# Merge gates and branch products channel by channel: all of mixer A and then all of mixer B, in place of both mixers tile by tile

## The chip, the cores and the metric

The kernel runs on one core of a Trainium2 chip. Its engines work side by side and in order: PE multiplies matrices, DVE, ACT and POOL work on vectors, SP issues the DMAs. The metric is the device time of one execution in microseconds; the kernel before takes 485.16 us (median of three runs, 485.05 to 486.32).

## The reference

A decoder layer with two token mixers over 512 tokens and 1,024 channels, all in float32. Cut to what matters here:

```python
h = rms_norm(x, norm_w[l])
proj = h @ w_in[l]          # q, k, v, z of both mixers, and gate_m (2 x 1024 channels)
o_a = moba_mixer(...)       # block sparse attention, 8 heads
o_b = nsa_mixer(...)        # compressed, selected and window attention, 8 heads
y_a = o_a * jax.nn.silu(z_a)
y_b = o_b * jax.nn.silu(z_b)
g_m = jax.nn.sigmoid(gate_m)
merged = g_m[..., :D_MODEL] * (y_a @ w_branch_a[l]) + g_m[..., D_MODEL:] * (y_b @ w_branch_b[l])
x = x + merged @ w_out[l]
```

What the change touches is the line with `merged`: 16 gate tiles of 128 channels (8 for A, 8 for B), each a product of the normed input with 128 columns of `w_in`, and 16 branch tiles, each a product of y_a or y_b (512 channels) with 128 columns of a branch weight.

## The kernel before

Every operand is split into a high and a low part in a 4-byte matmul format, and each product is three matmuls (high by high, low by high, high by low). The helper `mm3` (L314) issues them all, so nearly every product has the line L325 and is told apart by its result tile: pgt and pgc are projections, pbr is a branch product, po the output product. A gate tile is 8 chunks of the input, so 24 matmuls of 512 columns; a branch tile is 4 chunks of y, so 12 matmuls.

The program is written by a planner that runs when the kernel is built. It keeps a clock of its own and four generators that yield the cost of what they issue: `attention`, `gemms`, `cmp` and `x_rms`. The main loop (L1281) lets the ready generator with the least time so far go on, and delays what follows a product (chains of steps on DVE, ACT and POOL) until the modelled result is there. So PE's order is a mixture of attention and of the projections: where the attention waits for a softmax, products of `gemms` stand between. A generator that waits for something (`need`, `room`, a chain's `ready`) is passed over until the planner's clock has reached it. When attention has nothing but its own steps left and `gemms` is waiting, PE's order holds attention alone.

Attention is 24 units: 8 heads of mixer A, then 16 of mixer B (two for each head, of which the second adds to the first one's result O). A unit has scores (sps, L845 and L846), DVE's addition of the bias with a running minimum (L864), ACT's exponential (L879), DVE's reciprocal (L882), POOL's scaling of the probabilities P (L883), transposes on PE (pt, L892), the split into ph on ACT (L904) and pl on DVE (L906), and the products O with the values (L926). The products of a unit stand beside the scores of the next. After a head, ACT and DVE copy O out (ot L951, ys L955); after two heads DVE and ACT multiply by the silu gate and split the result (L965 to L967): the tiles yh and yl. Four pairs of them make up y of a mixer.

`gemms` (L1176) gives the projections in a fixed order, the z gates last. Then come the gates and branches. A gate (`gmgate`) is `gemm_chan` (24 matmuls into a PSUM buffer of the pool "g", which has two), then on DVE a multiplication with the token's norm (L1156) and on ACT a tanh (L1157). A branch is 12 matmuls into another buffer of "g" and DVE's (g + 1) * pbr (L1222), for which it needs all four y of its mixer. When both branches of a tile j are there, DVE adds them (L1226), ACT and DVE split the sum (L1227, L1228) into mh and ml, and after the last j the output product po runs.

Before: five gates of A first (`NGM = 5`). Then for every j: the gates of j that are still missing (B's, and from j = 5 on A's too), the branch of A, the branch of B, the sum.

Weights come through a stream `W` in the order in which the products use them: one DMA per tile of 256 KB, a split into wh (ACT or POOL, L296 or L298) and wl (DVE or POOL, L300). `ahead` (L493) sets how many tiles are split ahead, up to four.

Of the kernel before, what the change touches and what calls it, by code (L numbers as in the profile page):

```python
# [15 lines left out]
ALU = mybir.AluOpType  # L16
# [3 lines left out]
D = 1024  # L20
DH = 64
P = 128
# [12 lines left out]
POFF = [0, 128, 384, 768]  # L35
WT = 560
NATT = 35
NGM = 5
NW = 8
NRAW = 4  # L40
NWARM = 28
# [46 lines left out]
def hybrid_kernel(ctx: ExitStack, tc: tile.TileContext, x, xT, norm_w, wtok, wchan, gains, w1,  # L88
# [14 lines left out]
    def nm(s):  # L103
        uid[0] += 1
        return f"{s}{uid[0]}"
# [4 lines left out]
    now = [0.0]  # L110
# [26 lines left out]
    def cm(n):  # L137
        return 4.5 + 0.4427 * n
# [94 lines left out]
    def psum(tag, name, dt=F32):  # L233
        return alloc(tag, name, dt=dt)
# [9 lines left out]
    def room(*tags):  # L244

        def f():
            r = 0.0
            for tag in tags:
                if len(held[tag]) >= RES[tag][1]:
                    t = [z[0] for z in held[tag] if z[0] is not None]  # L250
                    if not t:
                        return None
                    r = max(r, min(t))
            return r
        return f

    def need(*names):
        def f():
            t = [done.get(n) for n in names]
            return None if None in t else max(t)  # L260
        return f
# [52 lines left out]
    def mm3(dst, sts, mvs, rows=1, start=True, stop=True):  # L314

        n = len(sts)
        cost = cm(dst.shape[-1]) * rows
        for k in range(0, n, rows):
            ks = range(k, k + rows)
            cs = {id(z[2]): z[2] for i in ks for z in (sts[i], mvs[i]) if z[2]}.values()  # L320
            if cs:
                yield all_of(*cs)
            for a, b in ((0, 0), (1, 0), (0, 1)):
                for i in ks:
                    nc.tensor.matmul(dst, sts[i][a], mvs[i][b], start=(start and i == a == b == 0),  # L325
                                     stop=(stop and i == n - 1 and b == 1))
                if rows > 1 or b:
                    yield cost if rows > 1 else 3 * cost
# [143 lines left out]
    def chan_tiles(name):  # L472
        return [(wchan[cnames.index(name), i], 512) for i in range(2)]
# [3 lines left out]
    tiles = []  # L477
    for n_ in ORDER_T:
        tiles += tok_tiles(n_) if n_ in tlay else chan_tiles(n_)
    for j in range(NGM):  # L480
        tiles += chan_tiles(f"gm{j}")
    for j in range(8):
        for w in range(2):
            if w or j >= NGM:
                tiles += chan_tiles(f"gm{8 * w + j}")
        tiles += [(wbr[j, i], 512) for i in range(2)]
    for c in range(4):
        tiles += [(wout[c, i], 512) for i in range(4)]
    W = Stream(tiles, NRAW - 1, lambda: wp.tile([P, WT], F32R, name=nm("wh"), tag="whi"),
               lambda: wp.tile([P, WT], F32R, name=nm("wl"), tag="wlo"))  # L490
    W1 = Stream([(w1[kv, q], 512) for kv in range(2) for q in range(8)], 1, lambda: att("vh"), lambda: att("vl"))

    def ahead(f):  # L493

        W.split(W.i + min(4, int(f * 4 + 0.8)))
# [442 lines left out]
    yhl = {}  # L938
# [211 lines left out]
    gms = {}  # L1150

    def gmgate(w, j):
        t = att("gm", F32)

        def emit(ps):
            c = Chain(now[0] + 230).do({"D": 602}, lambda e: e.tensor_mul(t, ps, R), ps)  # L1156
            gms[w, j] = t, c.do({"A": ca(512)}, lambda e: e.activation(t, t, AF.Tanh, scale=0.5))  # L1157
        yield from gemm_chan(f"gm{8 * w + j}", emit)

    def load_consts():  # L1160
        c = Chain(dma(ident, consts[:, :P], 512))
        c.do({"P": 547}, lambda e: e.tensor_copy(identr, ident)).mark("ident")
        dma(gn, bass.AP(tensor=gains.tensor, offset=gains.offset, ap=[[0, P], [1, 6 * DH]]), 1536)
        dma(rel, relone[:, :16], 64)
        o = alloc("gmt", "oh", (64, S))
        oh.append(att("oh"))
        c = Chain(dma(o, relone[:, 16:], 1024))
        c.do({"A": ca(512)}, lambda e: e.copy(oh[0][:64, :], o), o)
        c.do({"A": ca(16)}, lambda e: e.copy(relr, rel))
        c.do({"D": 82}, lambda e: e.tensor_sub(relr[32:64, :], rel[32:64, :], relr[32:64, :].bitcast(F32))).mark("oh")  # L1170
        t = dma(cst[:, P:], consts[:, P:], 2000)
        c = Chain(t)
        for i in (0, 2):
            c.do({"D": 102}, lambda e, i=i: e.tensor_scalar_mul(gn[:, i, :], gn[:, i, :], 0.125))

    def gemms():  # L1176
        yield from proj_v("v0", True)
        yield from proj_norm("qk0", 0, "ttgg")
        yield from bias_rows()
        yield from x_rows()  # L1180
        yield from proj_norm("qk1", 0)
        yield from compress_w(0)
        yield from compress_w(1)
        yield from proj_norm("qk2", 0)
        yield from proj_v("v1")
        yield from proj_norm("qk3", 0)
        yield from proj_norm("qb0", 2)
        yield from proj_norm("kb", 4)
        yield from proj_v("vb")
        yield from zgate("a", 0)  # L1190
        yield from zgate("a", 1)
        yield from proj_norm("qb1", 2)
        yield from zgate("a", 2)
        yield from zgate("a", 3)
        for j in range(4):
            yield from zgate("b", j)
        for j in range(NGM):
            yield from gmgate(0, j)
        xr = {}
        ms = []  # L1200
        for j in range(8):
            for w in range(2):
                if (w, j) not in gms:
                    yield from gmgate(w, j)
            ws = W.take(2, P)
            if j == 6:
                for t in range(0, NT, 2):
                    yield room("P")
                    xp = alloc("P", "xr", (P, 1280))
                    for i in range(2):  # L1210
                        xr[t + i, 0] = xp[:, i * 512:(i + 1) * 512]
                        dma(xr[t + i, 0], x[(t + i) * P:(t + i + 1) * P, :512], 2048)
            c = []
            for w in range(2):
                yield need(*((("y", "ab"[w], k) for k in range(4))))
                yield room("g")
                ps = psum("g", "pbr")
                yield from mm3(ps, ws[4 * w:4 * w + 4], [yhl["ab"[w], k] for k in range(4)])
                ahead((w + 1) / 2)
                g, gc = gms[w, j]  # L1220
                yield gc.ready
                c.append(Chain(max(now[0] + 230, gc.t)).do({"D": 602}, lambda e, g=g, ps=ps: e.scalar_tensor_tensor(  # L1222
                    g, g, 1.0, ps, op0=ALU.add, op1=ALU.mult), ps))
            g0, g1, a, b = gms[0, j][0], gms[1, j][0], att("mh"), att("ml")
            ch = c[1]
            ch.do(either(512), lambda e, g0=g0, g1=g1: e.tensor_add(g0, g0, g1))  # L1226
            ch.do({"A": ca(512)}, lambda e, g0=g0, a=a: e.copy(a, g0))  # L1227
            ch.do(either(512), lambda e, g0=g0, a=a, b=b: e.tensor_sub(b, g0, a.bitcast(F32)))  # L1228
            ms.append((a, b, ch))
        for c in range(4):  # L1230
            ws = W.take(4, 256)
            if c == 0:
                for t in range(NT):
                    xr[t, 1] = att("xr", F32)
                    dma(xr[t, 1], x[t * P:(t + 1) * P, 512:], 2048)
            st = [[(a[:, t * P:(t + 1) * P], b[:, t * P:(t + 1) * P], ch) for a, b, ch in ms] for t in range(NT)]
            pss_ = {}
            for t in range(NT):
                if c == 0 and t == 0:

                    for i in range(2):
                        yield room("g")
                        pss_[i] = psum("g", "po")
                        yield from mm3(pss_[i][:, :256], st[i][:7], ws[:7], stop=False)
                if t in pss_:
                    yield from mm3(pss_[t][:, :256], st[t][7:], ws[7:], start=False)
                    ps = pss_[t]
                else:
                    yield room("g")
                    ps = psum("g", "po")  # L1250
                    yield from mm3(ps[:, :256], st[t], ws)
                ahead((t + 1) / NT)
                xv = xr[t, c // 2][:, (c % 2) * 256:(c % 2 + 1) * 256]
                ch = Chain(now[0] + 230).do({"D": 335}, lambda e, xv=xv, ps=ps: e.scalar_tensor_tensor(
                    xv, ps[:, :256], 0.25, xv, op0=ALU.mult, op1=ALU.add), ps)
                ch.call(lambda t=t, c=c, xv=xv: dma(out[t * P:(t + 1) * P, c * 256:(c + 1) * 256], xv, 1024))
# [24 lines left out]
    while any(r.live for r in runs):  # L1281
        live = [r for r in runs if r.live]
        ws = [(r, r.wait()) for r in live]
# [86 lines left out]
```

## Time and profile before

| | |
|---|---|
| median of three runs | 485.16 us (485.05 to 486.32) |
| profiled execution | 486.89 us, of which the span is 485.1 us |
| mean granted clock of PE | 0.996 |
| busy: PE / DVE / ACT / POOL | 475.4 / 338.4 / 256.6 / 159.0 us |
| chain that ended last | PE 95%, DVE 2%, DMA 1% |

The profile is one execution. Busy time is a share of the whole span. Ends of matmuls are modelled, so that a 512-column matmul is shown with 0.39 us while the next one starts 0.23 us after it: the pace of PE is read from the starts. The chain of waits follows the work that ended last backwards, and its pieces add up to the span. A wait names the instruction that came last of those waited for.

### The profile page before, as it was taken

To read this page: it belongs to the slowest core of one execution; us is meant where nothing else is said; L and a number is where in the kernel's file an instruction comes from. 1 tells how busy PE (TensorE), PEld (TensorE's weight loads), DVE (VectorE), ACT (ScalarE), POOL (GpSimd) and SP (SyncE) were. 2 spreads that over 40 slices of the span, in tenths; PEclk is the share of its full clock that TensorE was granted. 3 is DMA by queue.
4 is the path that set the end of the run, shared out by engine and by line. 5 is a ranking of instruction groups with operands and counts; after the bars stand their busy time and mean duration, and the time that the engine had idled before them with its cause. 6 is when DMAs were issued, how large, how long until landed. Compare 5 with 4: busy or idle time off the path is not lost.

```text
span 485.1 us, 8685 instructions
## 1 busy us (share of the span) xinstructions
PE 475.4 (98%) x3060; PEld 426.7 (88%) x3060; DVE 338.4 (70%) x862; ACT 256.6 (53%) x631; POOL 159.0 (33%) x211
## 2 busy tenths in 40 slices
PE   7999999999999999999999999998999999999997
PEld 7999899999999989888888888886788888889997
DVE  5888999688898589797788677775555535444331
ACT  7656695477675286766686477764222231222210
POOL 0165577165555025465440254354000000000000
PEclk9999999999999999999999999998999999999999
DMA  8737243544344224122212221211133324526421
GB/s 275 221 74 171 61 134 112 151 114 135 79 123 140 74 66 113 41 65 68 65 45 75 84 68 57 49 42 45 43 106 112 94 81 139 166 76 217 142 89 43
DMA packets 28124, 49.15 MB, mean 101 GB/s; under 512 B 3313, under 2 KB 5745, under 8 KB 28081
## 3 DMA queue, kind: packets, MB, share of 16 engines
q1 hardware_dynamic: 28080, 48.60, 34.8%
q8 instruction: 24, 0.39, 0.4%
q14 instruction: 20, 0.16, 0.1%
HBM read 45.84 MB, written 2.75 MB: 100 GB/s over the span
## 4 chain that ended last, share of the span: by engine, by line
PE 95%; DVE 2%; DMA 1%; issue 0%; ACT 0%; POOL 0%; SPq 0%; DVEq 0%
PE pgc L325 30%; PE pgt L325 21%; PE po L325 9%; PE pbr L325 9%; PE O L926 6%; PE pt L892 6%; PE sps L845 3%; PE sps L846 3%; PE pgf L523 3%; PE pq L777 2%; PE hps L692 1%; DMA wr<-in_wtok 1%; PE hps L691 1%; PE scp L1014 1%; PE O L1070 0%
## 5 line engine op out<-in xcount | busy, mean ns | idle before, releaser
L300 DVE TENSOR_TENSOR wl<-wr,wh 128x512 fp32r<-128x512 f32 (+1 forms) x118 | 83.0, 712 | 7.3 <-ACT wh L296 7.0
L325 PE MATMUL pgc<-hh,wh 128*128 128x512 f32 x208 | 84.5, 406 | 0.0
L325 PE MATMUL pgt<-wh,hh 128*128 128x256 f32 (+1 forms) x288 | 82.6, 287 | 0.3 <-DVE v L608 0.3
L325 PE MATMUL pgc<-hh,wl 128*128 128x512 f32 x208 | 81.9, 394 | 0.0
L325 PE MATMUL pgc<-hl,wh 128*128 128x512 f32 x208 | 81.8, 393 | 0.0
L325 PE MATMUL pgt<-wl,hh 128*128 128x256 f32 (+1 forms) x288 | 81.2, 282 | 0.0
L325 PE MATMUL pgt<-wh,hl 128*128 128x256 f32 (+1 forms) x288 | 81.0, 281 | 0.0
L296 ACT CAST wh<-wr 128x512 fp32r<-128x512 f32 (+1 forms) x90 | 54.0, 616 | 27.5 <-DMA wr<-in_wout 21.9
L883 POOL TENSOR_SCALAR P<-P,sst,gate 128x512 f32<-128x512 f32 (+3 forms) x56 | 40.5, 727 | 62.8 <-DVE sst L882 46.8
L298 POOL TENSOR_SCALAR wh<-wr 128x512 fp32r<-128x512 f32 (+1 forms) x34 | 23.3, 687 | 114.9 <-DMA wr<-in_wchan 70.3
L864 DVE CUSTOM_DVE_ANT_0 sb<-sps,T 128x512 f32<-128x512 f32 (+3 forms) x96 | 46.0, 484 | 17.7 <-PE sps L846 16.6
L325 PEld LDWEIGHTS pgt<-wh,hh 128*128 128x128 f32 x288 | 54.3, 188 | 1.2 <-DVE v L608 0.5
L325 PEld LDWEIGHTS pgt<-wh,hl 128*128 128x128 f32 x288 | 54.2, 188 | 0.3
L325 PEld LDWEIGHTS pgt<-wl,hh 128*128 128x128 f32 x288 | 54.3, 188 | 0.0
L879 ACT ACTIVATE P<-sb,sst 128x512 f32<-128x512 f32 (+3 forms) x88 | 50.9, 580 | 6.3 <-DVE sst L864 6.0
L904 ACT CAST ph<-pt 128x512 fp32r<-128x512 f32 (+2 forms) x72 | 33.5, 477 | 26.0 <-PE pt L892 25.3
L325 PEld LDWEIGHTS pgc<-hl,wh 128*128 128x128 f32 x208 | 39.1, 188 | 9.1
L325 PEld LDWEIGHTS pgc<-hh,wh 128*128 128x128 f32 x208 | 39.1, 188 | 6.8
L325 PEld LDWEIGHTS pgc<-hh,wl 128*128 128x128 f32 x208 | 39.2, 188 | 6.7
L892 PE MATMUL pt<-cst,P 128*128 128x128 f32 x232 | 41.8, 278 | 0.3 <-POOL P L883 0.3
L906 DVE TENSOR_TENSOR pl<-pt,ph 128x512 fp32r<-128x512 f32 (+2 forms) x72 | 38.5, 548 | 4.1 <-ACT ph L904 3.7
L370 POOL TENSOR_TENSOR nr<-nss,mhalf 128x4 f32<-128x4 f32 x28 | 32.3, 1157 | 21.4 <-DVE nss L369 19.4
(208 smaller groups left out, 1076.6 us busy)
## 6 DMA issues: line engine op xcount, KB each, us to landing
wr<-in_wchan SPq DMA_DIRECT2D x52, 256.0 KB, 2.7
wr<-in_wtok SPq DMA_DIRECT2D x36, 256.0 KB, 2.8
T<-rtab SPq DMA_DIRECT2D x16, 256.0 KB, 3.8
wr<-in_w SPq DMA_DIRECT2D x16, 256.0 KB, 2.7
wr<-in_wbr SPq DMA_DIRECT2D x16, 256.0 KB, 2.6
wr<-in_wout SPq DMA_DIRECT2D x16, 256.0 KB, 2.9
x<-in_xT SPq DMA_DIRECT2D x8, 256.0 KB, 5.2
xr<-in_x SPq DMA_DIRECT2D x8, 256.0 KB, 4.4
```

The costliest lines, as they stand in the source:

```text
L296: e.copy(hi, raw)
L298: e.tensor_scalar(hi, raw, 1.0, 1.0, op0=ALU.mult, op1=ALU.mult)
L300: c.do(either(n), lambda e, hi=hi, lo=lo, raw=raw: e.tensor_sub(lo, raw, hi.bitcast(F32))).mark((w, 1, i))
L325: nc.tensor.matmul(dst, sts[i][a], mvs[i][b], start=(start and i == a == b == 0), stop=(stop and i == n - 1 and b == 1))
L370: c.do({"p": 430 + 150 * w}, lambda e: e.tensor_tensor(v(dst), v(ss), mhalf[:parts, :w], op=ALU.pow))
L864: e.tensor_tensor_reduce(z["sb"][:, :L], sps[:, :L], T[:, S - L:], scale=-1.0, scalar=3e38, op0=ALU.add, op1=ALU.min, accum_out=st[:, 0, b ...
L879: e.activation(pv(), z["sb"][:, :L], AF.Exp, bias=st[:, 0, b:b + 1], scale=-1.0, accum_out=st[:, 1, b:b + 1])
L883: c.do({"P": 315 + 0.834 * L}, lambda e: e.tensor_scalar(pv(), pv(), st[:, 2, b:b + 1], g, op0=ALU.mult, op1=ALU.mult))
L892: nc.tensor.transpose(pt[:, (b - kb) * P:(b - kb + 1) * P], u.p0 if u.p0 is not None and b == 0 else u.pb[:, POFF[b] + kb * P:POFF[b] + (k ...
L904: e.copy(z["w"][0], pt[:, :w])
L906: ch.do({"D": cd(w)}, lambda e: e.tensor_sub(z["w"][1], pt[:, :w], z["w"][0].bitcast(F32)), pt)
L926: nc.tensor.matmul(O[0][:, S - n:], v.bitcast(F32) if kb == 3 else v, w, start=(u.first and kb == 0 and i == 0), stop=(u.last and kb == 3 ...
```

## The change

The gates and branches of all eight tiles of mixer A come first, gate and branch in turn; then those of mixer B, each followed by the sum of its tile. The five gates ahead are gone. The branch is a generator function of its own. It takes one weight tile at a time instead of two, and calls `ahead` after each of its four chunks of y instead of once per branch. The weight stream has the same tiles in the new order. The numbers of instructions of each kind on PE stay as they are.

```diff
--- before.py
+++ after.py
@@ -35,7 +35,6 @@
 POFF = [0, 128, 384, 768]
 WT = 560
 NATT = 35
-NGM = 5
 NW = 8
 NRAW = 4
 NWARM = 28
@@ -477,13 +476,9 @@
     tiles = []
     for n_ in ORDER_T:
         tiles += tok_tiles(n_) if n_ in tlay else chan_tiles(n_)
-    for j in range(NGM):
-        tiles += chan_tiles(f"gm{j}")
-    for j in range(8):
-        for w in range(2):
-            if w or j >= NGM:
-                tiles += chan_tiles(f"gm{8 * w + j}")
-        tiles += [(wbr[j, i], 512) for i in range(2)]
+    for w in range(2):
+        for j in range(8):
+            tiles += chan_tiles(f"gm{8 * w + j}") + [(wbr[j, w], 512)]
     for c in range(4):
         tiles += [(wout[c, i], 512) for i in range(4)]
     W = Stream(tiles, NRAW - 1, lambda: wp.tile([P, WT], F32R, name=nm("wh"), tag="whi"),
@@ -1157,6 +1152,23 @@
             gms[w, j] = t, c.do({"A": ca(512)}, lambda e: e.activation(t, t, AF.Tanh, scale=0.5))
         yield from gemm_chan(f"gm{8 * w + j}", emit)
 
+    def branch(w, j):
+
+        ws = W.take(1, P)
+        yield need(*((("y", "ab"[w], k) for k in range(4))))
+        yield room("g")
+        ps = psum("g", "pbr")
+        i = 0
+        for c in mm3(ps, ws, [yhl["ab"[w], k] for k in range(4)]):
+            yield c
+            if not callable(c):
+                i += 1
+                ahead(i / 4)
+        g, gc = gms[w, j]
+        yield gc.ready
+        return Chain(max(now[0] + 230, gc.t)).do({"D": 602}, lambda e: e.scalar_tensor_tensor(
+            g, g, 1.0, ps, op0=ALU.add, op1=ALU.mult), ps)
+
     def load_consts():
         c = Chain(dma(ident, consts[:, :P], 512))
         c.do({"P": 547}, lambda e: e.tensor_copy(identr, ident)).mark("ident")
@@ -1194,15 +1206,13 @@
         yield from zgate("a", 3)
         for j in range(4):
             yield from zgate("b", j)
-        for j in range(NGM):
-            yield from gmgate(0, j)
         xr = {}
         ms = []
         for j in range(8):
-            for w in range(2):
-                if (w, j) not in gms:
-                    yield from gmgate(w, j)
-            ws = W.take(2, P)
+            yield from gmgate(0, j)
+            yield from branch(0, j)
+        for j in range(8):
+            yield from gmgate(1, j)
             if j == 6:
                 for t in range(0, NT, 2):
                     yield room("P")
@@ -1210,19 +1220,8 @@
                     for i in range(2):
                         xr[t + i, 0] = xp[:, i * 512:(i + 1) * 512]
                         dma(xr[t + i, 0], x[(t + i) * P:(t + i + 1) * P, :512], 2048)
-            c = []
-            for w in range(2):
-                yield need(*((("y", "ab"[w], k) for k in range(4))))
-                yield room("g")
-                ps = psum("g", "pbr")
-                yield from mm3(ps, ws[4 * w:4 * w + 4], [yhl["ab"[w], k] for k in range(4)])
-                ahead((w + 1) / 2)
-                g, gc = gms[w, j]
-                yield gc.ready
-                c.append(Chain(max(now[0] + 230, gc.t)).do({"D": 602}, lambda e, g=g, ps=ps: e.scalar_tensor_tensor(
-                    g, g, 1.0, ps, op0=ALU.add, op1=ALU.mult), ps))
+            ch = yield from branch(1, j)
             g0, g1, a, b = gms[0, j][0], gms[1, j][0], att("mh"), att("ml")
-            ch = c[1]
             ch.do(either(512), lambda e, g0=g0, g1=g1: e.tensor_add(g0, g0, g1))
             ch.do({"A": ca(512)}, lambda e, g0=g0, a=a: e.copy(a, g0))
             ch.do(either(512), lambda e, g0=g0, a=a, b=b: e.tensor_sub(b, g0, a.bitcast(F32)))
```

On PE, the order differs first behind gate 0 of mixer A (pgc_4018). Before:

```order
L325 MATMUL pgc_4018<-hh,wh_3942 128x512
L325 MATMUL pgc_4018<-hh,wl_3943 128x512
L325 MATMUL pgc_4018<-hl,wh_3942 128x512
L325 MATMUL pgc_4110<-hh,wh_4030 128x512
L325 MATMUL pgc_4110<-hh,wl_4031 128x512
L325 MATMUL pgc_4110<-hl,wh_4030 128x512
L325 MATMUL pgc_4110<-hh,wh_4030 128x512
```

After:

```order
L324 MATMUL pgc_4018<-hh,wh_3942 128x512
L324 MATMUL pgc_4018<-hh,wl_3943 128x512
L324 MATMUL pgc_4018<-hl,wh_3942 128x512
L324 MATMUL pbr_4109<-yh_2753,wh_4030 128x512
L324 MATMUL pbr_4109<-yh_2753,wl_4031 128x512
L324 MATMUL pbr_4109<-yl_2754,wh_4030 128x512
L324 MATMUL pbr_4109<-yh_2957,wh_4030 128x512
```

Before, the next product is gate 1 of A (pgc_4110); now it is branch 0 of A (pbr_4109), and gate 1 comes 12 matmuls later.

On PE, the last two attention units: the last product of the older one (pf), the transposes of the last one, its products, and its compressed part (ch). Before:

```order
L926 MATMUL O_4962<-pf_4971,vb_2659 128x128
L892 MATMUL pt_4986<-cst,p_4893 128x128
L892 MATMUL pt_4986<-cst,P_4900 128x128 x3
L892 MATMUL pt_4991<-cst,P_4900 128x128 x3
L892 MATMUL pt_4998<-cst,P_4900 128x128 x2
L926 MATMUL O_4962<-ph_4995,vb_2521 128x512
L926 MATMUL O_4962<-pl_4996,vb_2521 128x512
L892 MATMUL pt_5012<-cst,P_4900 128x128
L926 MATMUL O_4962<-ph_5001,vb_2572 128x384
L926 MATMUL O_4962<-pl_5002,vb_2572 128x384
L926 MATMUL O_4962<-ph_5004,vb_2612 128x256
L926 MATMUL O_4962<-pl_5005,vb_2612 128x256
```

After, from the older unit's last but one gate matmul on:

```order
L324 MATMUL pgc_4869<-hl,wh_4810 128x512
L921 MATMUL O_4980<-pf_4990,vb_2659 128x128
L887 MATMUL pt_4998<-cst,p_4907 128x128
L887 MATMUL pt_4998<-cst,P_4917 128x128 x3
L887 MATMUL pt_5003<-cst,P_4917 128x128 x3
L887 MATMUL pt_5010<-cst,P_4917 128x128 x2
L324 MATMUL pbr_5013<-yh_2753,wh_4849 128x512
L324 MATMUL pbr_5013<-yh_2753,wl_4850 128x512
L324 MATMUL pbr_5013<-yl_2754,wh_4849 128x512
L324 MATMUL pbr_5013<-yh_2957,wh_4849 128x512
L324 MATMUL pbr_5013<-yh_2957,wl_4850 128x512
L324 MATMUL pbr_5013<-yl_2958,wh_4849 128x512
```

Before, no gate or branch matmul stands here. Now three of a gate (pgc_4869, of which the last is shown) stand before the older unit's last product, and nine of branch 4 of A (pbr_5013, six are shown) behind the transposes. Three more follow before the last two products of attention. The last row of attention, ch, has the number 2065 on PE before and 2089 now.

On DVE, from the second but last scores of the last unit to its transposes' split: sb are scores, pl the low part of transposed probabilities, gm a gate, wl a weight's low part. Before:

```order
L864 ISA sb_4936,sst_4873<-sps_4924,T_4710 128x384
L864 ISA sst_4873 128x1
L906 TENSOR_TENSOR pl_4929<-pt_4919,ph_4928 128x512
L864 ISA sb_4954,sst_4873<-sps_4938,T_4710 128x256
L864 ISA sst_4873 128x1
L1222 SCALAR_TENSOR_TENSOR gm_4017<-gm_4017,pbr_4853 128x512
L906 TENSOR_TENSOR pl_4943<-pt_4932,ph_4942 128x384
L300 TENSOR_TENSOR wl_4951<-wr_4761,wh_4950 128x512
L882 RECIPROCAL sst_4873<-sst_4873 128x1
L906 TENSOR_TENSOR pl_4958<-pt_4945,ph_4957 128x256
L882 RECIPROCAL sst_4873<-sst_4873 128x1
L906 TENSOR_TENSOR pl_4996<-pt_4986,ph_4995 128x512
```

After:

```order
L859 ISA sb_4952,sst_4889<-sps_4940,T_4714 128x384
L859 ISA sst_4889 128x1
L901 TENSOR_TENSOR pl_4945<-pt_4935,ph_4944 128x512
L859 ISA sb_4967,sst_4889<-sps_4954,T_4714 128x256
L859 ISA sst_4889 128x1
L901 TENSOR_TENSOR pl_4959<-pt_4948,ph_4958 128x384
L877 RECIPROCAL sst_4889<-sst_4889 128x1
L901 TENSOR_TENSOR pl_4971<-pt_4961,ph_4970 128x256
L877 RECIPROCAL sst_4889<-sst_4889 128x1
L1151 TENSOR_TENSOR gm_4868<-pgc_4869,R 128x512
L901 TENSOR_TENSOR pl_5008<-pt_4998,ph_5007 128x512
```

Before, a branch's evacuation (gm_4017) and a weight split (wl_4951) stand between the last scores (sb_4954) and the last reciprocal; now neither does, and a gate's evacuation (gm_4868) stands behind the last reciprocal.

## Rows read from the trace of the kernel before

**Rows 1.** The page: busy us of PE, and the last chain by engine.
```profile
PE 475.4 (98%) x3060; PEld 426.7 (88%) x3060; DVE 338.4 (70%) x862; ACT 256.6 (53%) x631; POOL 159.0 (33%) x211
...
PE 95%; DVE 2%; DMA 1%; issue 0%; ACT 0%; POOL 0%; SPq 0%; DVEq 0%
```

**Rows 2.** The waits of PE over the whole span: total us, times, longest.
```profile
PE O L926 <- DVE pl L906: 1.3, 3, 0.6
...
PE pbr L325 <- ACT yh L966: 0.7, 1, 0.7
...
PE pt L892 <- POOL P L883: 0.3, 1, 0.3
```

**Rows 3.** Windows of 25 us: busy us (matmuls) by engine, granted clock, DMA.
```profile
300.00:325.00 25.00, 25.00 (x148) 21.88 (x146) 19.59 (x66) 18.34 (x54) 11.13 (x17) 1.00 0.21 54
325.00:350.00 25.00, 22.76 (x102) 17.51 (x101) 13.35 (x30) 10.73 (x25) 5.89 (x9) 0.93 0.13 43
350.00:375.00 25.00, 25.00 (x110) 20.30 (x109) 13.70 (x23) 5.61 (x10) 1.71 (x2) 1.00 0.33 95
```

**Rows 4.** Windows of 2 us, same columns.
```profile
334.00:336.00 2.00, 2.00 (x8) 1.32 (x7) 1.49 (x3) 0.98 (x4) 0.54 (x1) 0.53 0.00 0
```

**Rows 5.** Timeline of PE, 328 to 341 us: start, us, line, operation, [idle before it <-who ended it].
```profile
328.36 0.48 PE L926 MATMUL O<-ph,vb 128*128 128x512 f32 x1
329.08 0.50 PE L926 MATMUL O<-pl,vb 128*128 128x512 f32 x1 [0.24 <-DVE pl L906]
...
332.46 1.97 PE L892 MATMUL pt<-cst,P 128*128 128x128 f32 x8 [0.27 <-POOL P L883]
...
336.80 0.40 PE L325 MATMUL pbr<-yh,wh 128*128 128x512 f32 x1
...
340.79 0.39 PE L325 MATMUL pgc<-hh,wh 128*128 128x512 f32 x1
```

**Rows 6.** The chain of waits, 320 to 345 us: start, us, engine and line.
```profile
322.64 0.46 PE O L926 x2
...
323.34 0.11 PE pt L892
323.45 0.35 PE O L926 x2
...
324.49 0.46 PE O L926 x4
324.94 0.23 PE O L1070
...
327.02 0.44 PE pt L892 x4
...
331.21 1.21 POOL P L883 x2
...
340.95 4.19 PE pgc L325 x18
```

**Rows 7.** Timeline of DVE, 322 to 331 us.
```profile
322.58 0.68 DVE L1156 TENSOR_TENSOR gm<-pgc,R 128x512 f32<-128x512 f32 x1
...
329.28 0.68 DVE L1222 SCALAR_TENSOR_TENSOR gm<-gm,pbr 128x512 f32<-128x512 f32 x1
...
330.35 0.68 DVE L300 TENSOR_TENSOR wl<-wr,wh 128x512 fp32r<-128x512 f32 x1
```

**Rows 8.** Timeline of all engines, 428 to 444 us.
```profile
429.75 0.40 PE L325 MATMUL pbr<-yh,wh 128*128 128x512 f32 x1
...
429.95 0.69 DVE L1156 TENSOR_TENSOR gm<-pgc,R 128x512 f32<-128x512 f32 x1 [2.91 <-PE pgc L325]
...
438.05 0.39 PE L325 MATMUL po<-wl,mh 128*128 128x256 f32 x1 [0.24 <-DVE wl L300]
```

**Rows 9.** Instructions on gm: duration ns min/median/max, first and last start.
```profile
L1156 DVE TENSOR_TENSOR gm<-pgc,R x16: 627/692/693, 266.8 to 430.0; 128x512 f32<-128x512 f32 x16
...
L1222 DVE SCALAR_TENSOR_TENSOR gm<-gm,pbr x16: 681/689/690, 329.3 to 435.5; 128x512 f32<-128x512 f32 x16
```

## The prediction

> **What bounds the kernel now.** I read the page first, then the waits of PE, the windows, the timeline and the chain. The page shows a PE that is busy for 98% of the span, with 95% of the chain that ended last on it [rows 1]. So only time that PE loses can be won. The waits of PE name the losses: a product of probabilities and values, O, waiting for pl (three times), a branch product waiting for yh, a transpose waiting for P [rows 2]. All three lie between 325 and 345 us; the only other wait of any size is the start's, for the first weights, which the change does not reach. The windows show the same: from 325 to 350 us PE ran 102 matmuls at a granted clock of 0.93, in the next 25 us 110 at 1.00 [rows 3], and from 334 to 336 us the clock stood at 0.53, about the lower of its two levels, 1.2 GHz [rows 4].
>
> Recorded waits understate the loss, because a PE that idles between two starts counts as busy while the first drains. So I price the stretch by starts. It begins at 328.36, when the scores of the last attention unit are issued and nothing from the gate stream is left, and ends at 340.79, when the next gate starts: 12.43 us [rows 5]. Its content at full rate comes from the unit just before, which had filler [rows 6]. One set of products: 0.46 + 0.11 + 0.35 + 0.46 = 1.38 us. There are two sets, one of them with L1070 (0.23), so 2.99 us. Nine transposes at 0.44 / 4 = 0.11 us, 0.99 us. Twelve branch matmuls at 4.19 / 18 = 0.233 us each, 2.79 us. Sum 6.77 us. **The loss is 12.43 - 6.77 = 5.7 us**, in three parts: 328.36 to 332.46 (4.10 us against 1.38) loses 2.7, waiting for P; 332.46 to 336.80 (4.34 against 2.60) loses 1.7, waiting for pl and at the low clock; 336.80 to 340.79 (3.99 against 2.79) loses 1.2, waiting for the last y of mixer B.
>
> The cause is in the code. The gate stream runs beside attention as its filler. After gate (1,0) and branch (0,0) it meets branch (1,0), which needs all four y of B, and the last of these needs attention's last head. From then on attention runs alone on PE, one dependent step after the other.
>
> **The change part by part.** Nothing is removed or added: as many matmuls as before, the same gates, branches and weight tiles, the same arithmetic on DVE, ACT and POOL. Only places move. The order starts to differ behind gate 0 of A, whose result DVE takes at 266.8 us [rows 9]; nothing before that can change.
>
> 1. The branches of A become filler. They need y of A alone, finished with the eighth of 24 attention units. PE's order shows the end of attention after 24 more gate or branch matmuls than before (its last row of attention stands at 2089 instead of 2065): 24 x 0.233 = 5.6 us of work moved ahead, against a loss of 5.7 us. In before none stands between the last unit's scores and its last product. In after six stand between the scores and the older unit's products, three before the last unit's transposes, nine behind those and three before the last two products.
>
> 2. What is late next, by the three parts of the loss. For pl: nine matmuls, 2.1 us, stand where PE lost 1.7; nothing should remain. For y: gate 5 and branch 5 of A, gates and branches 6 and 7, and gate 0 of B stand before the first branch of B, 24 + 12 + 36 + 36 + 24 = 132 matmuls or 30.8 us; nothing remains. For P: it came 4.10 us after 328.36. In after PE has six matmuls, the older unit's products and three more matmuls in that place, 1.40 + 1.38 + 0.70 = 3.5 us. At the chain's present length 0.6 us would remain. But the chain should be shorter: in before DVE does a branch evacuation (0.68) and a weight split (0.68) inside it [rows 7], and in DVE's new order neither stands there. So 0 to 0.6 us; I take 0.2.
>
> 3. Evacuation. A gate or branch holds one of two PSUM buffers, so a gate's buffer must be free again 12 matmuls (2.8 us) after its end. In before this already happens at every j: the gate of B is followed by two branches, and the second takes the gate's buffer. DVE starts on it 0.2 us into the next product and needs 0.69 us [rows 8]; PE shows no wait there. Under attention DVE is later, but the 12 matmuls are spread over more time too: before the starved stretch the last gate was taken at 322.58 [rows 7], and no product waited for its buffer. Cost 0; if the cover were gone, each turn could cost up to one evacuation, 0.69 us.
>
> 4. DVE gets about three more evacuations of 0.68 us under attention and two more weight splits, some 3.4 us over the 60 us from 267 to 327 us, where over a fifth of it is free (19.59 of 25 us busy from 300 to 325) [rows 3]. The bounds: from 0 (PE does not wait for DVE there now) to the three waits of the last unit, 1.3 us [rows 2], in each of the eight units of the stretch, 10.4 us. I take 0.1, near the first: each unit keeps about as many gate and branch matmuls beside it by PE's order (before 48, 9, 18, 9, 15, 9, 18, 9, after 45, 9, 18, 9, 15, 12, 15, 15), so that the unit is no less covered.
>
> 5. Weights. One tile per 12 matmuls, in the same ratio as before for gates and branches; loads are only reordered. In the seam to the output product PE waits 0.24 us for a weight split [rows 8]. Now `ahead` runs after each quarter of a branch, so that on DVE three of the first four splits of the output weights stand ahead of the last branch's evacuation, where two stood. It may gain 0.24 us, or lose as much; I take a gain of 0.1.
>
> Sum: 5.7 - 0.2 - 0.1 + 0.1 = 5.5 us. The profiled execution took 486.89 us with a span of 485.1; the sum acts on the span, which becomes 479.6. The median of the runs is 485.16, so the forecast is **479.7 us**.
>
> A rule speaks against the new rhythm. The clock is 1.00 from 350 to 375 us, where one gate alternates with two branches [rows 3]. The Trainium skill ("TensorE: Matmul & The Clock Gate", "A second HAM failure mode: psum-queue depth-cycling") says that a stream of 512-column products which turns through PSUM buffers can idle briefly at every turn, and that the clock then falls again and again. By that the turns of one gate and one branch would cost clock from 341 to 435 us and the gain would be gone; by the row they cost nothing and the sum stands.
>
> **Rivals.** (a) *P stays late.* The chain from scores to P keeps its 4.1 us or grows, since POOL scales two tiles in a row (1.21 us) [rows 6] and the unit before must finish first; then PE idles, the clock falls as now, and only the parts for pl and y, 1.7 + 1.2, are won, less 0.3: 485.16 - 2.6 = 482.6. For it: it is the largest part of the loss. Against: nine matmuls stand in this place, and two steps less in the chain.
>
> (b) *DVE falls behind, the result is slower.* The new evacuations delay pl in the units that were covered so far. The price is point 4's upper end: 10.4 us in eight units, 485.16 - 5.5 + 10.4 = 490.1; in six units 487.5. It decides from (5.5 + 1.5) / 8 = 0.9 us a unit. For it: DVE is the busiest engine behind PE and works in order. Against: PE waits nowhere for it from 250 to 325 us, and the page's 70% leave room.
>
> (c) *The turns cost clock.* If from 341 to 435 us the clock were 0.93, as in the starved window [rows 3], the 94 us would grow by 0.07 x 94 = 6.6 us: 485.16 - 5.5 + 6.6 = 486.3, no difference that can be told. Against: 1.00 from 350 to 375 us, with the same two buffers and turns after 12 matmuls. This is the outcome that the Trainium skill's rule above would give.
>
> (d) *The change fills nothing*, because the planner holds the branches back: 485.2. The order excludes it, as far as an order can.
>
> **How the numbers follow.** Forecast 82%, with its own range of 478.9 to 481.3 (at best the whole 5.7 and the seam's 0.24, with 0.3 us for the spread of the sum; at worst P 0.4 us later still and one more unit with the last one's 1.3 us of waits). (a) 10%, (b) 5%, (c) 2%, (d) 1%. A measurement of this kernel tells about 0.3%, 1.5 us, from no change. Forecast and (a) are faster: 0.92. (c), (d) and a mild (b): same 0.04. The rest of (b): slower 0.04. The range that holds eight in ten takes in (a) as well: 478.8 to 482.8.
>
> **What would show it.** Right: the waits of PE for pl, P and yh between 325 and 345 us are gone or below 0.5 us in sum; the granted clock is 1.00 in every window there; the chain has pgc and pbr where POOL P, ot, ys and yh stood; the span ends near 479.6. Step 2 is wrong if a transpose still waits for P; step 3 if pgc or pbr waits for an evacuation of gm; step 4 if O waits for pl before 315 us. The forecast as a whole is wrong if the clock drops behind 341 us or new waits of PE exceed 1 us in sum.

## The result, and the profile after

The changed kernel takes 480.76 us (median of four runs, 479.29 to 481.04) against 485.74 us (485.05 to 487.58): a ratio of 0.9881 with a 95% interval of 0.9858 to 0.9904. Beside the experiments it ran once more: 480.38 us against 485.83 us, ratio 0.989 (0.9871 to 0.9909). Both say 5.0 to 5.5 us, a good 1%. The forecast was 479.7 us.

The page of the changed kernel, the lines that answer to [rows 1]:

```profile
span 478.9 us, 8690 instructions
...
PE 471.8 (99%) x3060; PEld 425.8 (89%) x3060; DVE 339.0 (71%) x862; ACT 254.8 (53%) x628; POOL 159.7 (33%) x214
...
PE 97%; DVE 1%; DMA 1%; ACT 0%; SPq 0%; issue 0%; DVEq 0%
```

Its waits of PE, all of them (who waited for whom: us in total, times, longest), to be held against [rows 2]:

```profile
PE pgf L518 <- ACT wh L295: 2.1, 1, 2.1
PE pw L385 <- POOL ones L337: 0.9, 1, 0.9
PE pgt L324 <- DVE v L603: 0.3, 1, 0.3
PE hps L687 <- DVE vl L299: 0.2, 1, 0.2
PE po L324 <- DVE xr L1253: 0.2, 1, 0.2
```

The three waits of the starved stretch, for pl, yh and P, are gone, and so is the wait for a weight split in front of the output product [rows 8]. What is left stands in front of the stretch or behind it. The windows (busy us and matmuls by engine, granted clock, DMA) that answer to [rows 3]:

```profile
325.00:350.00 25.00, 25.00 (x129) 21.04 (x128) 14.24 (x31) 10.70 (x27) 5.65 (x10) 1.00 0.25 76
350.00:375.00 25.00, 25.00 (x110) 20.36 (x109) 11.11 (x17) 5.61 (x10) 1.85 (x3) 1.00 0.33 95
```

From 325 to 350 us PE now runs 129 matmuls where it ran 102, at a granted clock of 1.00 in place of 0.93. The chain of waits through the last attention unit (start, us, engine and line), which in before ran through DVE, POOL and ACT [rows 6]:

```profile
329.12 0.12 PE sps L841
329.24 0.22 PE pt L887 x2
329.46 1.39 PE pgc L324 x6
330.86 0.46 PE O L921 x2
331.32 0.11 PE pt L887
331.43 0.59 PE O L921 x4
332.02 0.70 PE pgc L324 x3
332.72 0.22 PE O L921 x2
332.94 0.98 PE pt L887 x9
333.93 2.09 PE pbr L324 x9
336.01 0.46 PE O L921 x2
...
338.08 0.24 PE O L1065
338.32 5.55 PE pgc L324 x24
```

Every piece is PE's, each starts where the one before it ends, and nine transposes take 0.98 us, where the prediction counted 0.99. From the start of the first product to the start of what follows attention's last one, what took 8.44 us without filler in before (328.36 to 336.80) takes 7.46 us here, with fifteen filler matmuls inside (330.86 to 338.32). The seam to the output product runs through as well:

```profile
427.04 2.76 PE pbr L324 x12
429.80 5.34 PE po L324 x45
```

### The profile page after: what moved, and what is told of

It is laid out like the page before. It is cut to its first block, busy times and chain, and to the rows that moved or that the text cites. A ratio compares the mean times of both kernels' runs of the same rounds, so it can differ in the third digit from the quotient of the medians.

```text
span 478.9 us, 8690 instructions
## 1 busy us (share of the span) xinstructions
PE 471.8 (99%) x3060; PEld 425.8 (89%) x3060; DVE 339.0 (71%) x862; ACT 254.8 (53%) x628; POOL 159.7 (33%) x214
## 4 chain that ended last, share of the span: by engine, by line
PE 97%; DVE 1%; DMA 1%; ACT 0%; SPq 0%; issue 0%; DVEq 0%
PE pgc L324 30%; PE pgt L324 21%; PE po L324 9%; PE pbr L324 9%; PE O L921 6%; PE pt L887 6%; PE sps L840 3%; PE sps L841 3%; PE pgf L518 3%; PE pq L772 2%; PE hps L687 1%; PE hps L686 1%; DMA wr<-in_wtok 1%; PE scp L1009 1%; PE O L1065 0%; PE pct L1052 0%
## 5 line engine op out<-in xcount | busy, mean ns | idle before, releaser
L299 DVE TENSOR_TENSOR wl<-wr,wh 128x512 fp32r<-128x512 f32 (+1 forms) x118 | 84.2, 717 | 10.3 <-ACT wh L295 10.1
L295 ACT CAST wh<-wr 128x512 fp32r<-128x512 f32 (+1 forms) x87 | 51.9, 617 | 25.1 <-DMA wr<-in_wout 19.3
L887 PE MATMUL pt<-cst,P 128*128 128x128 f32 x232 | 40.7, 272 | 0.0
```

What stands on the lines that cost most here:

```text
L295: e.copy(hi, raw)
L299: c.do(either(n), lambda e, hi=hi, lo=lo, raw=raw: e.tensor_sub(lo, raw, hi.bitcast(F32))).mark((w, 1, i))
L887: nc.tensor.transpose(pt[:, (b - kb) * P:(b - kb + 1) * P], u.p0 if u.p0 is not None and b == 0 else u.pb[:, POFF[b] + kb * P:POFF[b] + (k ...
```

## The experiments

Two theories stood. *Filler*: the gain is the work that PE can do while attention's last units wait for their own steps. *Rhythm*: the gain comes from gate and branch in turn, with weights taken one tile at a time. The first four kernels leave the rhythm of before as it is and change only what stands in reach of attention. For each, the stretch that the edits can touch is read from two starts: the last matmul of the compressed scores (scp, in front of the first difference) and the first output product (po). Up to scp PE's order is the same in all these kernels, and still that start differs by up to 2 us between executions, so the stretch behind it is finer than the whole time. The first four were timed beside the kernel before in the table's first row, the last four and the changed kernel beside one of 485.83 us (484.26 to 486.1); each ratio is to the one beside it.

| kernel | time, us (range) | ratio to before (95%) | last scp to first po, us |
|---|---|---|---|
| before | 485.64 (484.63 to 486.93) | | 435.3 - 261.9 = 173.4 |
| changed, again | 480.38 (479.68 to 480.57) | 0.989 (0.9871 to 0.9909) | 429.1 - 261.6 = 167.5 |
| four gates ahead | 489.14 (488.56 to 490.27) | 1.0071 (1.0047 to 1.0096) | 437.1 - 261.0 = 176.1 |
| six gates ahead | 482.49 (482.16 to 483.53) | 0.9929 (0.9904 to 0.9954) | 431.8 - 261.9 = 169.9 |
| eight gates ahead | 479.88 (479.2 to 481.19) | 0.9881 (0.9854 to 0.9908) | 428.8 - 260.9 = 167.9 |
| B reads y of A | 480.35 (479.94 to 481.18) | 0.989 (0.9867 to 0.9913) | 428.9 - 261.4 = 167.5 |
| B first | 503.03 (502.87 to 503.19) | 1.0359 (1.0331 to 1.0387) | 451.6 - 260.9 = 190.7 |
| evacuation in two steps | 479.34 (478.91 to 480.48) | 0.9879 (0.9855 to 0.9903) | 427.9 - 260.2 = 167.7 |
| split ahead once | 481.09 (480.69 to 481.86) | 0.9909 (0.9889 to 0.9929) | 428.1 - 260.5 = 167.6 |

**Four, six and eight gates ahead**, in the kernel before:

```diff
-NGM = 5
+NGM = 4      # and 6, and 8
```

> The kernel before with four gates of mixer A ahead of the tiles instead of five; the rhythm of gate, gate, branch, branch stays. Theory (filler): attention's end now stands 24 matmuls earlier on PE (last row 2041, before 2065), so the last two units run with no gate or branch matmul beside them instead of one; 24 x 0.233 = 5.6 us more are left for after it, and PE idles for as long: 5.6 us slower than before, up to 8 where the lower clock lasts longer, 490.5 to 494 us. Rival (rhythm: the gain comes from gate and branch in turn, one weight tile at a time, in the stretch after attention): that rhythm is as in before, so no change, 485 to 486 us.

> The kernel before with six gates of mixer A ahead instead of five. Theory (filler): attention's last row moves to 2089 as in the changed kernel, 24 matmuls stand between the last scores and it, so the waits for P and pl go. But the first branch of B stands right behind attention, so the wait for the last y (1.2 us) stays: 485.5 - 4.4 = 481.1 us, 480.5 to 482. Rival (rhythm): no change, 485 to 486 us.

> The kernel before with all eight gates of mixer A ahead; gate, branch, branch behind. Theory (filler): 24 matmuls between the last scores and attention's last row, and more than 24 behind it ahead of the first branch of B, so all three waits go: as fast as the changed kernel, 479.3 to 480.8 us, with a span near 479. Rival (rhythm): no change, 485 to 486 us, since the branches still stand in pairs with two weight tiles at a time.

One constant moves the time from 489.1 over 485.6 and 482.5 to 479.9 us, and with eight gates ahead the kernel before is as fast as the changed one. The rhythm is out: nothing of it was changed. Two sizes were missed. With four gates it lost 3.5 us and not 5.6. Its waits of PE:

```profile
PE pt L892 <- POOL P L883: 3.4, 3, 1.7
...
PE O L926 <- DVE pl L906: 1.1, 4, 0.4
```

PE waited longer, but attention also ended sooner: its last product (L1070) starts at 333.0, 72.0 us after the last scp, in before at 336.5, 74.6 us after it. Of these 2.6 us, 0.8 are the clock's: it fell in before and did not fall here. Here is its window (granted clock 1.00), and then PE's transposes of the last unit's P and the first matmul behind attention:

```profile
325.00:350.00 25.00, 23.04 (x109) 17.85 (x110) 13.70 (x29) 9.20 (x22) 3.43 (x6) 1.00 0.13 42
```

```profile
329.79 1.09 PE L892 MATMUL pt<-cst,P 128*128 128x128 f32 x8 [0.26 <-POOL P L883]
...
333.32 0.40 PE L325 MATMUL pbr<-yh,wh 128*128 128x512 f32 x1
```

These are the same matmuls as in before, alone on PE in both. They take 3.53 us here (329.79 to 333.32) and took 4.34 in before (332.46 to 336.80, [rows 5]), so of the 1.7 us that the prediction's second part loses, 0.8 belong to the low clock and 0.9 to the waits. What is left of the 2.6 us, 1.8, is filler that had only held attention up. So a missing filler matmul costs its time only where the chain beside it is the longer one.

With six gates the waits for P and pl are gone and one wait is left, for the last y, with more than it had cost in before: the twelve matmuls of B's first branch take 4.86 us from start to start (338.08 to 342.94), a loss of 2.1 us where before lost 1.2. The end of attention in its chain of waits:

```profile
338.43 1.29 DVE wl L300 x2
339.72 0.03 issue
339.75 0.69 DVE ys L955
340.45 0.02 issue
340.47 0.70 DVE ys L965
341.18 0.02 issue
341.20 0.63 ACT yh L966
341.82 0.04 issue
341.87 1.23 PE pbr L325 x3
```

Two weight splits stand on DVE in front of the steps that make y, and only nine matmuls of B's first branch are behind attention to cover them. That is the price of filler that reaches only to attention's last row: 482.5 in place of 479.9 us with two gates more.

**The branches of B read y of A**, in the kernel before:

```diff
-                yield need(*((("y", "ab"[w], k) for k in range(4))))
+                yield need(*((("y", "a", k) for k in range(4))))
...
-                yield from mm3(ps, ws[4 * w:4 * w + 4], [yhl["ab"[w], k] for k in range(4)])
+                yield from mm3(ps, ws[4 * w:4 * w + 4], [yhl["a", k] for k in range(4)])
```

> The kernel before, in which the branches of B read y of A (the output is then not the layer's: mixer B's attention is computed but not merged). Nothing else changes: five gates ahead, gate, branch, branch. Theory (filler): what stopped the stream of gates and branches was the need for y of B; without it the stream goes on under attention's tail and all 5.7 us of loss go: 479.3 to 480.8 us, no wait of PE for P, pl or yh. Rival (rhythm): no change, 485 to 486 us.

480.35 us, and no wait for P, pl or yh is left. All that was taken away is the need for mixer B's last head, so this need is what stopped the stream.

**B first**, in the changed kernel (the two loops and the weight stream change places):

```diff
         for j in range(8):
-            yield from gmgate(0, j)
-            yield from branch(0, j)
+            yield from gmgate(1, j)
+            yield from branch(1, j)
         for j in range(8):
-            yield from gmgate(1, j)
+            yield from gmgate(0, j)
...
-            ch = yield from branch(1, j)
+            ch = yield from branch(0, j)
```

> The changed kernel with the mixers swapped: gates and branches of all tiles of B first, then those of A. The rhythm and the number of instructions stay. Theory (filler): branch 0 of B waits for attention's end, so only one gate is left as filler for the last eight units, which had 165 matmuls of it (38 us) in the changed kernel and have 9 now; about 36 us of PE work moves behind attention. Each of these units then loses what the last one lost in the kernel before (2.7 + 1.7 us, more where the scores wait too): 480 + 8 x 4.4 = 515 us, 505 to 525. Rival (rhythm): as fast as the changed kernel, 479 to 481 us.

503.03 us: the same rhythm and the same instructions, 22.7 us slower than the changed kernel. The direction is the filler's; the size was set too high. Two views of it, the waits of PE and the windows:

```profile
PE pt L887 <- POOL P L878: 4.6, 7, 1.4
PE O L921 <- DVE pl L901: 3.5, 11, 0.6
PE pct L1052 <- DVE pcs L1039: 3.2, 1, 3.2
```

```profile
275.00:300.00 25.00, 20.53 (x118) 15.23 (x116) 19.53 (x75) 19.05 (x59) 10.07 (x17) 1.00 0.14 35
300.00:325.00 25.00, 20.26 (x110) 14.68 (x109) 17.00 (x59) 16.15 (x50) 9.77 (x17) 1.00 0.00 1
```

The waits for P and pl come back all along the row of units and not only in the last; the one for pct stands once, in front of the row. Attention's last product starts at 322.6, 61.7 us after the last scp, in the changed kernel run beside it at 337.3, 75.6 us after it. So 156 matmuls or 36.3 us of work were taken out and attention ran 13.9 us faster without them: 22.4 us of loss, close to the measured 22.7. The expectation had priced each unit by the last one, which is alone on PE; inside the row, the next unit's scores still stand beside it, which is read from the order and was not tested by itself.

**The branch's evacuation in two steps**, in the changed kernel:

```diff
-        return Chain(max(now[0] + 230, gc.t)).do({"D": 602}, lambda e: e.scalar_tensor_tensor(
-            g, g, 1.0, ps, op0=ALU.add, op1=ALU.mult), ps)
+        c = Chain(max(now[0] + 230, gc.t)).do({"D": 602}, lambda e: e.tensor_scalar_add(g, g, 1.0))
+        return c.do({"D": 602}, lambda e: e.tensor_mul(g, g, ps), ps)
```

> The changed kernel with the branch's evacuation on DVE in two instructions (g + 1, then times the product) instead of one: 16 more DVE instructions, up to 0.69 us each, some 5 of them under attention. Theory (filler): DVE has more than a fifth of its time free there, and PE is covered; within 0.5 us of the changed kernel, 479.3 to 481.3 us, and no wait of PE for gm, pl or P. Rival (DVE is close to its limit under attention, so that the moved evacuations are as many as it bears): five units lose up to 1.3 us each, 483 to 487 us.

479.34 us, with no wait of PE for gm, pl or P. It is no faster by its edit: the stretch behind scp is 167.7 us, the changed kernel's 167.5, and its profiled execution reached scp 1.4 us earlier, in front of all that the edit touches. Up to attention's last product DVE bears four more steps (0.41 to 0.97 us each) than in the changed kernel, so the rival in which DVE falls behind is out.

**Split ahead once at a branch's end**, in the changed kernel:

```diff
             if not callable(c):
                 i += 1
-                ahead(i / 4)
+        ahead(1)
```

> The changed kernel with the weight stream asked to split ahead once at the end of each branch (four tiles) instead of after each quarter of it. Theory: the quarters matter only at the seam to the output product, where the kernel before waited 0.24 us for a weight split; at most that wait comes back, 479.3 to 481.3 us. Rival (weights: the steadier splitting of weights carries a good part of the gain): over 1.5 us slower than the changed kernel, with waits of PE for wl or wh, 482 us or more.

481.09 us, 0.7 us over the changed kernel beside it (480.69 to 481.86 against 479.68 to 480.57). Its waits of PE have a line that neither the changed kernel nor, in this size, the kernel before has:

```profile
PE po L324 <- DVE wl L299: 1.1, 1, 1.1
```

The stretch up to the first po is unchanged (167.6); the loss stands behind it, where the output product's weights are split too late. From the first po to the one that waits for DVE's residual sum (xr) it takes 7.36 us (428.09 to 435.45), in the changed kernel beside it 6.00 (429.06 to 435.06). That is 1.4 us, over five times the 0.24 that the theory allowed; the medians show half of it. So the weight stream matters at this one place and does not carry the gain. The edit also moved attention's end: 21 more filler matmuls stand in front of its last product, which starts 80.5 us after scp (75.6 in the changed kernel), and the stretch up to po did not change by that.

**The changed kernel again**, for the three beside it:

> The changed kernel once more, for the comparison on the same chip with the three runs beside it: 479.3 to 481 us, 4.7 to 6.7 us faster than before.

480.38 us, as expected.

**The kernel before, twice more**, one profile each:

> The kernel before once more, for one question: how much of the 5.7 us of loss that were read from one execution is the low clock (0.53 from 334 to 336 us there) and how much the waits. If the clock stays at 1.00 in the stretch, the theory that the waits alone carry most of the loss expects 4.7 us from the last scores to the next gate in excess of the work (the second part 0.7 us instead of 1.7), a span 1 us shorter. Rival: the low clock is most of the second and third part, and the loss falls to 3 us. If the clock falls again, the same 5.7 us as before.

> The same as the run beside it: with the clock at 1.00 in the stretch, a loss of 4.7 us by the theory and of 3 us by the rival; with the clock low again, 5.7 us.

By themselves inconclusive: 486.75 and 487.26 us, and the clock fell in both. From the second of them:

```profile
334.00:336.00 2.00, 2.00 (x7) 1.30 (x6) 1.49 (x3) 0.91 (x4) 0.62 (x1) 0.50 0.00 0
```

The starved stretch took 12.44 us in both (328.17 to 340.61, 328.71 to 341.15), 12.43 in the first profile: the loss of 5.7 us repeats. What share of it is the clock's is seen from the four gates above, where it did not fall: 0.8 us. So 4.9 us belong to the waits, close to the theory's 4.7 and far from the rival's 3.

## Why the prediction was right

*The cause and step 1 (filler).* Shown from both sides: more filler of another kind gives the same gain (eight gates), taking the need away gives it too (B reads y of A), and less filler costs time (four gates, B first). Each sign that the prediction named is there: no wait for pl, P or yh, the clock at 1.00, PE's own products in the chain, and a span of 478.9 us where 479.6 was forecast. The stretch from scp to po became 5.9 us shorter (173.4 to 167.5), where 5.7 of loss were read and 24 x 0.233 = 5.6 us of work moved.

*Step 2 (what is late next).* Right for pl and y. For P, 0.2 us were kept and nothing is left. POOL's rows of the changed kernel, the scaling that ends the chain:

```profile
330.86 1.20 POOL L878 TENSOR_SCALAR P<-P,sst,gate 128x384 f32<-128x384 f32 x2 [1.58 <-DVE sst L877]
```

The last scores and the transposes that ask for P, in the changed kernel:

```profile
328.96 0.28 PE L841 MATMUL sps<-kx,qs 128*128 128x256 f32 x1
...
332.89 1.04 PE L887 MATMUL pt<-cst,P 128*128 128x128 f32 x8
```

The last scores in before, to be held against POOL's row there [rows 6]:

```profile
328.11 0.28 PE L846 MATMUL sps<-kx,qs 128*128 128x256 f32 x1
```

P is ready at 332.06, 3.1 us after the last scores' start (328.96), in before at 332.41, 4.3 us after it (328.11). The shorter chain on DVE that the order showed is worth 1.2 us, and PE asks for P only at 332.89. Rival (a), that P stays late, is out.

*Step 3 (evacuation) and step 4 (DVE).* No wait for either in the changed kernel, nor with two DVE steps for each branch. The 0.1 us kept for DVE was not needed.

*The rule against it.* The clock is 1.00 in every window from 341 to 429 us, where gate and branch turn through two buffers; the failure that the Trainium skill ("TensorE: Matmul & The Clock Gate", "A second HAM failure mode: psum-queue depth-cycling") describes, there of a bf16 kernel, is not seen, and rival (c) is out.

*Step 5 (weights).* Taken as +0.1, and it is about 0.5: from the first po to the one that waits for DVE's residual sum (441.78 and 435.64 us) it was 6.48 us (from 435.30) and is 6.00 (from 429.64). With eight gates, where the weights are split ahead as in before, it is 6.47 (428.81 to 435.28).

*The term that was mis-sized is the loss itself, as a median.* The sum came out at 5.5 us; between profiled executions the span fell by 6.2 (485.1 to 478.9), between medians by 5.0 and 5.5. The first 5.7 us were read from an execution in which the clock fell, and 0.8 us of them are the clock's. Not every run of before may have that: of the 14 timed beside the experiments, six show a granted clock of 0.999 or 1.000 and spans of 482.5 to 484.3 us (median 483.15), eight show 0.993 to 0.996 and 483.8 to 485.1 (median 484.15). The 1.0 us between them is close to the 0.8. But no trace shows where the clock fell in these runs, and a low mean alone does not tell it: two runs of the changed kernel have 0.996 too, and spans of 478.7 and 477.1 us beside 478.9 and 478.6 us at 1.000. In how many runs of before the 0.8 us are lost stays open. That the forecast lies so near the medians is in part luck: it takes a loss with the low clock in it from a median of runs that may not all have it, keeps 0.3 us for P and DVE that nothing took, and has the gain of step 5 about 0.4 us too small.

## What to carry to other kernels

When a stream of independent products runs beside a chain of dependent ones, order it by what each product needs: those that need the chain's end go last, and all others are kept as filler until that end. The filler has to reach past the chain's last matmul, for the steps of the other engines that make the result; and one matmul less costs its time only where the chain is longer than the work beside it. Read the loss from starts: the recorded waits of the starved stretch came to 2.3 us and the loss was 5.7, of which the low clock made 0.8.

## What the runs showed of the hardware

The clock does not follow idle time in any simple way. With four gates PE idled more than in before (3.4 us for P alone), and in that execution the granted clock stood at 1.00 through the whole stretch; with B first it was 1.00 from 275 to 325 us although PE was busy for only 20.5 and 20.3 of each 25 us, with waits of up to 1.4 us. There it did fall earlier, directly behind a wait of 3.2 us (for pct, which starts at 268.87):

```profile
270.00:272.00 2.00, 2.00 (x12) 1.90 (x11) 1.59 (x4) 0.95 (x3) 0.00 (x0) 0.50 0.00 0
```

In the kernel before it fell to the lower level in all three profiles, at the same place, behind recorded waits of at most 0.6 us. Executions also differ by 2 us before the first instruction that any edit touches, though PE's order is the same up to there: the last scp starts between 260.2 and 262.2 us in the profiles above. A difference of 1 us between two of these kernels is better read from a stretch of the trace than from the whole time.
